# Single PSUM banks for the maxima of each FoX head, earlier loads of the FoX weights, and w_out's blocks subtracted on VectorE

## The chip, the cores and the metric

One core of one Trainium2 chip runs the whole program. The metric is the device time of one execution in microseconds (us); lower is better. The engines are named as in the profile: PE is TensorE's matmuls, PEld its weight loads, DVE is VectorE, ACT is ScalarE, POOL is GpSimd, SP is SyncE, whose queue issues every DMA of this kernel.

## The reference

One decoder layer over 2048 tokens of width 1024, with 16 learned meta tokens ahead of them. Three mixers (FoX attention, GLA, RG-LRU) read one input projection, and an output projection follows:

```python
hn = rms_norm(h, pre_g[l])
proj = hn @ w_in[l]
(fq, fk, fv, ff, fg, gq, gk, gv, ga, gg, lx, lg) = split_projection(proj)
...
# FoX: 8 heads of 64; c = cumsum(log_sigmoid(ff + b_f))
s = jnp.einsum('bhqd,bhkd->bhqk', qi, kf) * scale + cqi[..., None] - c[:, :, None, :]
mask = (kpos[None, :] <= qpos[:, None]) & valid[None, :]
p = jax.nn.softmax(jnp.where(mask, s, NEG), axis=-1)
y_fox = jnp.einsum('bhqk,bhkd->bhqd', p, vf) * jax.nn.silu(fg)
...
y = jnp.concatenate([y_fox, y_gla, y_lru], axis=-1) * vmask
h = h + rms_norm(y @ w_out[l], post_g[l])
```

## The kernel before, in words

The program is one long list of jobs in a fixed order: GLA (two pairs of heads, four chunks of 512 tokens each), RG-LRU (eight blocks of 128 channels), FoX (four pairs of heads, p = 0 to 3, four chunks of 512 queries each, c = 0 to 3), then the output projection. `merge` interleaves two generators: the mixing part of one job (for FoX `fox_attend`) and the preparing part of the next (`fox_prepare`). A scheduler then turns this list into one order for each engine by its own model of the time; each engine runs its order strictly in turn. Tiles come from rings of a fixed number of buffers; a new tile waits until the last reader of the tile whose place it takes is done.

The layout of FoX. The two heads of a pair lie on the upper and lower 64 partitions of the tiles KA (keys, high and low half), QA (queries) and KX. A product over one head's 64 channels therefore uses one half of the rows of PE's 128 x 128 array, and the products of the two heads use different halves.

`fox_prepare` projects keys (`fox_keys`), queries and values (`fox_values`, 24 matmuls of 128 x 128 for each block, line 503) and computes, for each block of 128 queries (i = 0 to 3) and each chunk pc of keys up to the diagonal, the largest score of each query: two products of the heads into the PSUM tile `mq` (line 1224), on the diagonal a mask added by a matmul (line 1228), and one reduction for each head on DVE (line 1232), which adds the decays CB and takes the maximum. `mq` is a tile of two banks, one bank for each head, and there is one such tile. The maxima of a chunk are transposed through the bank `fx` (line 1244), split on ACT and DVE and sent into QA by six small DMAs (line 1255).

`fox_attend` computes for each block j of 128 keys the scores of both heads (line 1284, six products with KA and two with KX; line 1290 the mask), the exponential on ACT into `pt` (line 1292), running sums `za` on DVE and POOL (lines 1296 to 1300), and the product with the values into the bank `fv` (line 1308; float32, the two heads in different halves of the columns of the array). At the end of a chunk the sums go through `fx` (line 1319) and through HBM to the normaliser `rz` (lines 512 to 521, 1326), POOL multiplies (lines 1315, 1327) and the result is stored to `yD` (line 1328).

Weights. Each group of 128 columns of w_in is loaded as a `raw` tile of 512 KB (line 418, ring of 4), squared and summed on ACT (line 465), and converted to two float16 halves on ACT and DVE (lines 436, 437) by `load_end`, which `post` calls at the start of the next job. For FoX the load of fk and fv of the next pair is in the list at chunk 0, its squares at chunk 1; fq and fg at chunks 2 and 3; each of these DMAs is queued behind `k.mark`, the last store to `yD` or the last of the six DMAs into QA, whichever the list had last.

Beside FoX runs `wout_ready`, in steps spread over the sixteen FoX jobs: it loads w_out in 32 blocks `wr` (256 KB) for their squares, loads them again, subtracts blocks from one another (`minus`, line 1381, 32 of 128 x 512), and converts them into the staging tile `ws` (lines 1447, 1448), which is stored to `wD` (line 1388). The output projection reads `wD`.

Of the kernel before, what the change touches and what calls it, by code (L numbers as in the profile page):

```python
# [9 lines left out]
F32 = mybir.dt.float32  # L10
# [6 lines left out]
ALU = mybir.AluOpType  # L17
# [70 lines left out]
class Ctx:  # L88
# [6 lines left out]


BUFS = {"A0": 3, "A2": 3, "KA": 6, "KB": 6, "QA": 2, "QB": 2, "B0": 2, "B1": 2, "B2": 2, "B3": 2, "V": 6, "G": 2, "R": 1,
        "T": 3, "ZZ": 8, "WR": 8, "WT": 2, "WS": 3, "TS": 12, "WC": 1, "OO": 3, "OX": 2, "LV": 5, "AT": 2, "AC": 2, "GV": 6, "GG": 6, "GS": 6, "M": 1, "MV": 1, "YG": 2, "RS": 2, "ZS": 1, "ZA": 2, "PT": 6, "ED": 2, "KT": 1, "Z": 1, "WH": 1, "WL": 1, "XC": 4, "X": 16, "L0": 4, "L1": 4, "L2": 2, "L3": 2, "L4": 6}


def unit(k, tag, shape, dt=F32, name=None):
# [8 lines left out]
    return ap  # L110


PBUFS = {"pj": 2, "mx": 2, "st": 2, "pv": 2, "fx": 1, "fv": 1}


def bank(k, tag="pj"):
# [292 lines left out]
def load_begin(k, nm):  # L409
    load_dma(k, nm)  # L410
    load_squares(k)


def load_dma(k, nm):
    cols, src = (48, k.ins["w_fa"]) if nm == "fa" else (P, k.ins["w_grp"][GROUPS[nm]])
    raw = k.wp.tile([P, KT, P], F32, name="raw", bufs=RAWB)[:, :, 0:cols]
    with k.tc.issue_after(k.mark) if nm[0] in ("fk", "fv", "fq", "fg") else nullcontext():
        k.nc.sync.dma_start(out=raw, in_=src)
    k.sent.append((nm, raw, cols))

# [20 lines left out]
def post(k, n=1):  # L441

    while k.begun:
        load_end(k)
    for _ in range(min(n, len(k.todo))):
        nm = k.todo.pop(0)
        if nm is None:
            load_squares(k)
        elif nm[0] == "load":
            load_dma(k, nm[1])  # L450
        else:
            load_begin(k, nm)


def fox_loads(p):

    return {0: [("load", ("fk", p)), ("load", ("fv", p))], 1: [None, None],
            2: [("load", ("fq", p)), ("load", ("fg", p))], 3: [None, None]}


def squares(k, tiles, scale=1.0):
# [647 lines left out]
def fox_begin(k, p):  # L1109

    nc = k.nc
    d = k.st["k", p] = Ctx()
    d.hi, d.lo, d.cb, d.V = [], [], [], []
    d.x = k.wk.tile([P, SEQ], BF16, name="KX", tag="KX", bufs=2)
    last = unit(k, "M", [P, 7 * NM], name="last")
    d.last = [last[:, NM // 2 * i:NM // 2 * (i + 1)].bitcast(F16) for i in range(2)]
    lx = last[:, NM:NM // 2 * 3].bitcast(BF16)
    lc = last[:, NM * 2:NM * 4].rearrange("p (h t) -> p h t", h=2)
    with k.tc.issue_after(k.pool):
        nc.gpsimd.memset(d.x, 1.0)  # L1120
# [12 lines left out]
    d.x = [d.x[:, CH * c:CH * c + CH] for c in range(NCH)] + [lx]
# [35 lines left out]
def fox_values(k, p, c):  # L1169
    nc = k.nc  # L1170
    wv = k.w["fv", p]
    m, nb = (P, 4) if c < NCH else (NM, 1)
    V = unit(k, "V" if c < NCH else "MV", [m, nb, P], name="fv")
    ps = blocks(bank(k))
    for i in range(nb):
        proj_tm(k, ps[0:m, i, :], wv, CH * c + P * i, m)
        yield
    nc.scalar.activation(V[0:m, :, :], ps[0:m, 0:nb, :], AF.Copy, scale=wv[2][0:m])
    k.st["k", p].V.append(V)
# [12 lines left out]
def fox_prepare(k, p, c):  # L1192
# [23 lines left out]
    for i in range(4):  # L1216
        for pc in range(c + 2 if i == 3 else c + 1):
            n = NM if pc > c else CH if pc < c else min(CH, NM + P * (i + 1))

            d0, d1, off = (P - NM, P, 0) if pc > c else (0, min(P, CH - NM - P * i), NM + P * i)  # L1220
            ps = pair(k, "mq")
            for h in range(2):
                hs = slice(64 * h, 64 * h + 64)
                nc.tensor.matmul(out=ps[:, h, 0:n], lhsT=qh[hs, P * i:P * i + P], rhs=d.hi[pc][hs, 0:n],  # L1224
                                 start=True, stop=pc < c)
            for h in range(2):
                if pc >= c:
                    nc.tensor.matmul(out=ps[:, h, off:off + d1 - d0], lhsT=k.identb, rhs=k.triq[:, d0:d1],
                                     start=False, stop=True)
            for h in range(2):  # L1230
                junk = k.wk.tile([P, 2, CH], BF16, name="mj", tag="MJ", bufs=1)
                nc.vector.tensor_tensor_reduce(out=junk[:, h, 0:n], in0=ps[:, h, 0:n], in1=d.cb[pc][:, h, 0:n],  # L1232
                                               scale=1.0, scalar=-3e38, op0=ALU.add, op1=ALU.max,
                                               accum_out=mp[:, 4 * h + i, pc:pc + 1])
            yield
            if next(rest, 0) is None:
                yield
    mm = small(k, "mm", [P, 8], bufs=2)
    nc.vector.tensor_reduce(mm, mp, axis=AX.X, op=ALU.max)
    for _ in range(1):  # L1240
        if next(rest, 0) is None:
            yield
    ps = bank(k, "fx")
    nc.tensor.transpose(out=ps[0:8, 0:P], in_=mm, identity=k.ident)

    mr = k.wk.tile([8, P], F32, name="mr", tag="MR", bufs=1)
# [16 lines left out]
def fox_attend(k, p, c):  # L1263
# [49 lines left out]
    o = unit(k, "R", [P, CH], name="fo")  # L1313
    nc.scalar.copy(out=o, in_=pv)
    nc.gpsimd.tensor_tensor(o, o, gate, op=ALU.mult)
    zp = bank(k, "fx")
    for h in range(2):
        hs = slice(64 * h, 64 * h + 64)
        nc.tensor.matmul(out=zp[hs, :], lhsT=k.ones[:, 0:64], rhs=za[h], start=True, stop=True)
# [18 lines left out]
def wout_ready(k):  # L1338
# [35 lines left out]
    for i, (q, j) in enumerate(groups):  # L1374
        (b11, b12, b22, b21), ahead = ahead, []
        if i + 1 < len(groups):
            ahead = [load(groups[i + 1][0], b, groups[i + 1][1]) for b in (0, 2, 3, 1)]

        def minus(x, y):
            t = k.wk.tile([P, KT // 2, P], F32, name="wt", tag="WT", bufs=BUFS["WT"])  # L1380
            nc.gpsimd.tensor_tensor(t, x, y, op=ALU.subtract)
            return t

        def put(nm, x):
            hl = stage()
# [261 lines left out]
```

## Time and profile before

| | |
|---|---|
| median of 3 runs | 2018.9 us (2014.85 to 2019.87) |
| the profiled execution, its own time | 2016.83 us |
| its span from the first to the last instruction | 2015.1 us |
| mean granted clock of TensorE | 0.976 of full speed |
| busy share of PE / DVE / ACT / POOL | 94% / 63% / 50% / 31% |
| from the first `mq` product to the first product of the output projection | 899.0 to 1702.2 us |

A share is busy time over the span. PE's busy time counts a matmul from its start to its modelled end. "Idle before" in a row is the time in which the engine had nothing to run before that instruction, with the instruction whose end let it go on.

### The profile page before, as it was taken

The page shows a single profiled execution, that of the slowest core. Times are in us where ns is not written, and L with a number is a line of the kernel's source. Part 1 is how long each engine was busy: PE and PEld are TensorE (multiplying, and loading weights), DVE is VectorE, ACT ScalarE, POOL GpSimd, SP SyncE. Part 2 cuts the span into 40 slices and gives each one's busy share as a digit, 9 for nine tenths or more (in the row PEclk, how much of TensorE's full clock was granted, in tenths as well). Part 3 has the DMA queues.
Part 4 walks back from the last instruction along what each step waited for, and adds up shares of the span by engine and source line. Part 5 has one row for each costly group of instructions (what it writes and reads, how often), then busy time and mean ns, then how long its engine had stood idle before and what let it go on. Part 6 is the DMA issues. An engine that isn't in the chain of part 4 may idle for free.

```text
span 2015.1 us, 39446 instructions
## 1 busy us (share of the span) xinstructions
PE 1893.3 (94%) x15988; PEld 985.4 (49%) x15988; DVE 1265.8 (63%) x2802; ACT 1011.9 (50%) x1561; POOL 630.7 (31%) x596
## 2 busy tenths in 40 slices
PE   6888999999999999989989998999899998999998
PEld 5456666665555555555434442344335432444443
DVE  7666363445788778673665367746874675567764
ACT  7655553344888887752345333433443335444441
POOL 3434232322433344330112113322332124343432
PEclk9889899999999999999999999999999998999999
DMA  7200120211211110101131104321232108733411
GB/s 226 70 7 29 41 86 28 74 44 34 74 43 45 44 41 22 63 20 64 38 116 48 54 12 135 95 77 64 90 116 70 43 23 303 218 116 115 136 43 63
DMA packets 116135, 152.70 MB, mean 76 GB/s; under 512 B 18792, under 2 KB 75816, under 8 KB 115952
## 3 DMA queue, kind: packets, MB, share of 16 engines
q1 hardware_dynamic: 115952, 150.18, 23.4%
q8 instruction: 125, 2.05, 0.4%
q14 instruction: 58, 0.48, 0.1%
HBM read 108.71 MB, written 41.33 MB: 74 GB/s over the span
## 4 chain that ended last, share of the span: by engine, by line
PE 66%; DVE 8%; DMA 5%; ACT 5%; issue 4%; POOL 4%; SPq 1%; POOLq 0%; ACTq 0%; DVEq 0%
PE pj L491 26%; PE pj L1576 14%; PE pj L503 5%; PE fv L1308 5%; PE sq L1284 4%; PE mq L1224 2%; DMA raw<-in_w_grp_dram 2%; PE st L596 1%; DMA rz<-rowD 1%; DVE mj L1232 1%; PE gs L1034 1%; DMA rowD<-consts 1%; PE pv L1068 1%; DVE xc L569 1%; POOL v L618 1%
## 5 line engine op out<-in xcount | busy, mean ns | idle before, releaser
L491 PE MATMUL pj<-xhl,whl 128*128 128x512 f16 (+3 forms) x3960 | 808.9, 355 | 10.0 <-ACT whl L436 7.7
L491 PEld LDWEIGHTS <-whl 128*128 128x128 f16 x3984 | 363.9, 98 | 393.9 <-issue 68.5
L1292 ACT ACTIVATE pt<-sq,consts 128x1024 f32<-128x1024 f32 (+4 forms) x176 | 163.4, 928 | 255.2 <-PE sq L1290 101.9
L1300 POOL TENSOR_TENSOR za<-za,pt 128x512 f32<-128x512 f32 (+1 forms) x80 | 99.4, 1243 | 503.3 <-ACT pt L1292 442.3
L1232 DVE CUSTOM_DVE_ANT_0 mj<-mq,CB 128x512 bf16<-128x512 f32 (+4 forms) x344 | 189.5, 579 | 57.0 <-PE mq L1224 28.5
L1576 PEld LDWEIGHTS <-whl 128*128 128x128 f16 x1344 | 130.7, 98 | 161.2 <-issue 4.9
L503 PEld LDWEIGHTS <-xhl 128*128 128x128 f16 (+1 forms) x3264 | 191.3, 99 | 32.5 <-issue 28.2
L503 PE MATMUL pj<-whl,xhl 128*128 128x128 f16 (+1 forms) x3024 | 196.1, 223 | 0.0
L1300 DVE TENSOR_TENSOR za<-za,pt 128x512 f32<-128x512 f32 (+3 forms) x208 | 135.6, 675 | 91.8 <-ACT pt L1292 84.6
L1308 PE MATMUL fv<-pt,fv 128*64 128x512 f32 (+4 forms) x704 | 174.7, 534 | 0.6 <-DVE QA L1106 0.6
L1576 PE MATMUL pj<-xhl,whl 128*128 128x512 f16 x768 | 169.1, 381 | 0.0
L1284 PE MATMUL sq<-QA,KA 64*128 64x512 f16 (+4 forms) x1032 | 128.4, 345 | 14.3 <-ACT pt L1292 11.8
L1576 PE MATMUL pj<-ts,whl 128*128 128x512 f16 x576 | 125.7, 379 | 0.0
L569 DVE SCALAR_TENSOR_TENSOR xc<-lx,consts,xc 128x448 f32<-128x448 f32 (+1 forms) x120 | 94.0, 783 | 3.5
L1560 POOL TENSOR_TENSOR o<-o,xt 128x512 f32<-128x512 f32 x31 | 51.6, 1683 | 120.3 <-issue 91.7
L1542 ACT ACTIVATE sqo<-o 128x512 bf16<-128x512 f32 x32 | 20.1, 630 | 129.5 <-DVE o L1536 129.5
L527 ACT ACTIVATE gate<-pj,consts 128x512 f32<-128x512 f32 (+2 forms) x72 | 46.1, 641 | 71.6 <-PE pj L491 62.5
L1284 PEld LDWEIGHTS <-KA 64*128 64x128 f16 (+1 forms) x1032 | 40.6, 94 | 84.0 <-issue 62.0
L1224 PE MATMUL mq<-KA,QA 64*128 64x512 f16 (+4 forms) x344 | 61.4, 346 | 21.3 <-DVE consts L1232 19.1
L604 POOL TENSOR_TENSOR v<-a 128x448 f32<-128x448 f32 (+1 forms) x40 | 39.0, 976 | 134.1 <-ACT a L602 134.1
L1582 DVE SCALAR_TENSOR_TENSOR o<-pj,consts,o 128x512 f32<-128x512 f32 x56 | 41.0, 744 | 60.0 <-PE pj L1576 55.8
L1284 PE MATMUL sq<-QA,KX 64*128 64x512 bf16 (+4 forms) x344 | 66.6, 342 | 4.1 <-DMA QA<-dr 4.1
(253 smaller groups left out, 2810.8 us busy)
## 6 DMA issues: line engine op xcount, KB each, us to landing
raw<-in_w_grp_dram SPq DMA_DIRECT2D x44, 512.0 KB
wr<-in_w_out_dram SPq DMA_DIRECT2D x64, 256.0 KB
y<-yD SPq DMA_DIRECT2D x32, 512.0 KB
wD<-ws SPq DMA_DIRECT2D x56, 256.0 KB
CB<-c32D SPq DMA_DIRECT2D x32, 256.0 KB
xhl<-wD SPq DMA_DIRECT2D x16, 512.0 KB
xt<-in_x_dram SPq DMA_DIRECT2D x16, 512.0 KB
out_dram<-o SPq DMA_DIRECT2D x32, 256.0 KB
```

Of the source, the lines that this page charges most:

```text
L491: nc.tensor.matmul(out=ps, lhsT=a[:, kt, 0:m], rhs=b[:, kt, u0:u0 + n], start=i == 0, stop=i == 23)
L503: nc.tensor.matmul(out=ps, lhsT=a[:, kt, u0:u0 + m], rhs=b[:, kt, :], start=i == 0, stop=i == 23)
L527: k.act = nc.scalar.activation(out, ps, AF.Tanh, scale=hinv).ins
L569: nc.vector.scalar_tensor_tensor(out=xc, in0=lx[:, j:j + n], scalar=cw(j), in1=xc, op0=ALU.mult, op1=ALU.add)
L1224: nc.tensor.matmul(out=ps[:, h, 0:n], lhsT=qh[hs, P * i:P * i + P], rhs=d.hi[pc][hs, 0:n], start=True, stop=pc < c)
L1232: nc.vector.tensor_tensor_reduce(out=junk[:, h, 0:n], in0=ps[:, h, 0:n], in1=d.cb[pc][:, h, 0:n], scale=1.0, scalar=-3e38, op0=ALU.add, op ...
L1284: nc.tensor.matmul(out=sp[0:m, h, off:], lhsT=a[j // 4][hs, kk], rhs=b[hs, off:], start=i == 0, stop=i == 3 and d < 0)
L1292: k.exp = nc.scalar.activation(pt[0:m, :, off:], sp[0:m, :, off:], AF.Exp, scale=K.esc[0:m]).ins
L1300: eng.tensor_tensor(out=za[h][0:m, off:], in0=za[h][0:m, off:], in1=pt[0:m, h, off:], op=ALU.add)
L1308: nc.tensor.matmul(out=pv[hs, off1:], lhsT=V1[0:m1, j1 % 4, hs], rhs=pt1[0:m1, h, off1:], start=j1 == 0, stop=j1 == nj - 1)
L1560: eng.tensor_tensor(out=o, in0=o, in1=xt[:, h, :], op=ALU.add)
L1576: nc.tensor.matmul(out=ps, lhsT=a[:, kt, :], rhs=w[b + kt // 4][:, :, kt % 4, :], start=kt + j == 0, stop=(kt, j) == (KT - 1, 2))
```

## The change

`minus` runs on DVE in place of POOL. The rings of `wr` and `ws` shrink from 8 to 6 and from 3 to 2. FoX's weights get a ring of their own, `rawf`, of three tiles; load, squares and conversion of a group are asked for together (fk and fv at chunk 1, fq and fg at chunk 3), and only those of the first pair are queued behind `k.mark`. In `fox_prepare` each head takes a single bank of a ring of three named `mq`, from which the transposes of the maxima and the sums of `za` take their bank too; the two-bank tile and `fx` go. The values of the last 16 tokens move into the tile `last`.

```diff
-        "T": 3, "ZZ": 8, "WR": 8, "WT": 2, "WS": 3, ...
+        "T": 3, "ZZ": 8, "WR": 6, "WT": 2, "WS": 2, ...
...
-PBUFS = {"pj": 2, "mx": 2, "st": 2, "pv": 2, "fx": 1, "fv": 1}
+PBUFS = {"pj": 2, "mx": 2, "st": 2, "pv": 2, "mq": 3, "fv": 1}
...
-    raw = k.wp.tile([P, KT, P], F32, name="raw", bufs=RAWB)[:, :, 0:cols]
-    with k.tc.issue_after(k.mark) if nm[0] in ("fk", "fv", "fq", "fg") else nullcontext():
+    fox = nm[0] in ("fk", "fv", "fq", "fg")
+    raw = k.wp.tile([P, KT, P], F32, name="rawf" if fox else "raw", bufs=3 if fox else RAWB)[:, :, 0:cols]
+    with k.tc.issue_after(k.mark) if fox and nm[1] == 0 else nullcontext():
...
-    return {0: [("load", ("fk", p)), ("load", ("fv", p))], 1: [None, None],
-            2: [("load", ("fq", p)), ("load", ("fg", p))], 3: [None, None]}
+    return {1: [("fk", p), ("fv", p)], 3: [("fq", p), ("fg", p)]}
...
-            ps = pair(k, "mq")
+            ps = [bank(k, "mq") for _ in range(2)]
             for h in range(2):
                 hs = slice(64 * h, 64 * h + 64)
-                nc.tensor.matmul(out=ps[:, h, 0:n], lhsT=qh[hs, P * i:P * i + P], rhs=d.hi[pc][hs, 0:n],
+                nc.tensor.matmul(out=ps[h][:, 0:n], lhsT=qh[hs, P * i:P * i + P], rhs=d.hi[pc][hs, 0:n],
                                  start=True, stop=pc < c)
...
-    ps = bank(k, "fx")
+    ps = bank(k, "mq")
     nc.tensor.transpose(out=ps[0:8, 0:P], in_=mm, identity=k.ident)
...
-    zp = bank(k, "fx")
+    zp = bank(k, "mq")
...
-            nc.gpsimd.tensor_tensor(t, x, y, op=ALU.subtract)
+            nc.vector.tensor_tensor(t, x, y, op=ALU.subtract)
```

PE's order is the same up to the first chunk of FoX and through the output projection, and differs in between; the changed program's line numbers are 5 or 6 lower (line 418 alone is now 419). PE, the second step of the first chunk (272 keys), before: both heads, then both masks.

```order
L503 MATMUL pj<-whl,xhl 128x128
L1224 LDWEIGHTS QA
L1224 MATMUL mq<-KA,QA 128x272
L1224 LDWEIGHTS QA
L1224 MATMUL mq<-KA,QA 128x272
L1228 LDWEIGHTS consts
L1228 MATMUL mq<-consts 128x128
L1228 LDWEIGHTS consts
L1228 MATMUL mq<-consts 128x128
L503 LDWEIGHTS xhl
```

The same place now; the rows left out are 18 products of the values (`pj`, line 497).

```order
L1219 LDWEIGHTS QA
L1219 MATMUL mq<-KA,QA 128x272
L1223 LDWEIGHTS consts
L1223 MATMUL mq<-consts 128x128
L497 LDWEIGHTS xhl
L497 MATMUL pj<-whl,xhl 128x128
...
L1219 LDWEIGHTS QA
L1219 MATMUL mq<-KA,QA 128x272
L1223 LDWEIGHTS consts
L1223 MATMUL mq<-consts 128x128
```

The second head's product and mask have moved 18 products of the values behind the first head's. PE again, in the second chunk of the first pair, where `fox_attend` multiplies with the values, before: one row holds both heads (x2).

```order
L1290 LDWEIGHTS consts
L1290 MATMUL sq<-consts 128x128
L1308 MATMUL fv<-pt,fv 64x400 x2
L491 LDWEIGHTS whl
L491 MATMUL pj<-xhl,whl 128x512
```

The same place now.

```order
L1285 LDWEIGHTS consts
L1285 MATMUL sq<-consts 128x128
L1303 MATMUL fv<-pt,fv 64x400
L1219 LDWEIGHTS QA
L1219 MATMUL mq<-KA,QA 128x400
L1223 LDWEIGHTS consts
L1223 MATMUL mq<-consts 128x128
L1303 MATMUL fv<-pt,fv 64x400
L485 LDWEIGHTS whl
```

One head's maximum product and its mask now stand between the two heads' products with the values. Over the whole of FoX the program before has 176 pairs of heads at line 1224, of which one is not back to back, and 171 at line 1308, of which 24 are not; now 95 and 48 are not. The order of PE changes its kind of instruction (128 rows, 64 rows, 64 columns, float32 or not) 882 times before and 964 times now.

SP, where the loads of fk and fv of a later pair stand, before: behind the store of a chunk (line 1328).

```order
L521 DMA rowD<-consts 128x8
L1326 DMA rz<-rowD 64x512 x2
L1328 DMA yD<-fo 128x512
L418 DMA raw<-in_w_grp_dram 128x1024 x2
L1346 DMA wr<-in_w_out_dram 128x512 x6
```

Now one such pair of loads stands ahead of the normaliser's round trip.

```order
L1250 DMA QA<-dr 1x4x128 x6
L508 DMA rowD<-zs 1x512 x2
L419 DMA rawf<-in_w_grp_dram 128x1024 x2
L510 DMA consts<-rowD 128x8
L515 DMA rowD<-consts 128x8
```

No load of these now follows a store of line 1323 directly, and seven of the sixteen stand ahead of the first of the six DMAs into QA, where four did.

## Rows read from the trace of the kernel before

**Rows 1.** The page, busy time of each engine, share of the span, count.

```profile
span 2015.1 us, 39446 instructions
PE 1893.3 (94%) x15988; PEld 985.4 (49%) x15988; DVE 1265.8 (63%) x2802; ACT 1011.9 (50%) x1561; POOL 630.7 (31%) x596
```

**Rows 2.** Windows: length, busy us (count) by engine, clock, DMA share, GB/s.

```profile
899.00:1702.00 803.00, 754.39 (x5605) 321.78 (x5603) 488.25 (x1339) 310.99 (x455) 195.79 (x153) 0.98 0.25 80
```

**Rows 3.** Waits of PE in 899:1702: total us, times, longest.

```profile
PE mq L1224 <- DVE consts L1232: 19.1, 20, 3.4
PE sq L1284 <- ACT pt L1292: 11.8, 13, 3.6
PE sq L1284 <- DMA QA<-dr: 4.1, 3, 2.4
...
PE pj L491 <- DVE whl L437: 0.2, 1, 0.2
```

**Rows 4.** Timeline of PE at 935.0 and 1475.2: start, us, shape.

```profile
935.04 0.39 PE L1224 MATMUL mq<-KA,QA 64*128 64x512 f16 x2
935.36 0.62 PE L503 MATMUL pj<-whl,xhl 128*128 128x128 f16 x8
...
1475.20 0.89 PE L503 MATMUL pj<-whl,xhl 128*128 128x128 f16 x13
1476.02 0.39 PE L1284 MATMUL sq<-QA,KX 64*128 64x512 bf16 x1
1476.34 0.82 PE L491 MATMUL pj<-xhl,whl 128*128 128x512 f16 x3
```

**Rows 5.** Timeline of PE at 1501.2 and 1510.3 (line 1308: two records a product).

```profile
1501.28 0.82 PE L1284 MATMUL sq<-QA,KA 64*128 64x512 f16 x6
1501.94 0.38 PE L1284 MATMUL sq<-QA,KX 64*128 64x512 bf16 x2
1502.25 1.08 PE L1308 MATMUL fv<-pt,fv 128*64 128x512 f32 x4
1503.26 0.34 PE L503 MATMUL pj<-whl,xhl 128*128 128x128 f16 x3
...
1510.79 1.07 PE L1308 MATMUL fv<-pt,fv 128*64 128x512 f32 x2
1511.79 0.61 PE L1284 MATMUL sq<-QA,KA 64*128 64x512 f16 x4
```

**Rows 6.** The chain that ended last, 1425:1450: start, us, what.

```profile
1433.96 0.33 SPq L1328
...
1434.39 4.37 DMA raw<-in_w_grp_dram
...
1440.00 1.01 ACT pt L1292
...
1441.05 1.04 PE sq L1284 x8
```

**Rows 7.** Timeline of PE, the instructions after five waits [idle before].

```profile
1024.68 0.61 PE L1284 MATMUL sq<-QA,KA 64*128 64x512 f16 x4 [3.03 <-ACT pt L1292]
1139.89 0.29 PE L1224 MATMUL mq<-KA,QA 64*128 64x272 f16 x2 [1.34 <-DVE consts L1232]
1232.26 0.41 PE L1224 MATMUL mq<-KA,QA 64*128 64x272 f16 x2 [3.37 <-DVE consts L1232]
1348.26 0.29 PE L1224 MATMUL mq<-KA,QA 64*128 64x272 f16 x2 [2.42 <-DVE consts L1232]
1441.05 0.39 PE L1284 MATMUL sq<-QA,KA 64*128 64x512 f16 x2 [3.63 <-ACT pt L1292]
```

**Rows 8.** Groups by form in 899:1702: busy us, mean ns, idle before.

```profile
L1300 DVE TENSOR_TENSOR za<-za,pt 128x512 f32<-128x512 f32 x120 | 99.2, 850 | 52.2 <-ACT pt L1292 45.4 <-POOL za L1300 6.2
...
L1381 POOL TENSOR_TENSOR wt<-wr 128x512 f32<-128x512 f32 x16 | 24.1, 1508 | 4.4 <-DMA wr<-in_w_out_dram 4.4
L1381 POOL TENSOR_TENSOR wt<-wr,wt 128x512 f32<-128x512 f32 x16 | 23.5, 1467 | 0.3
...
L1297 DVE TENSOR_TENSOR za<-pt 128x512 f32<-128x512 f32 x24 | 15.5, 687 | 21.3 <-ACT pt L1292 21.3
...
L512 ACT COPY zs<-fx 128x512 f32<-128x512 f32 x15 | 8.8, 586 | 20.7 <-PE fx L1319 20.7
```

More of the change, by code (lines that the diff above doesn't have):

```diff
@@ L97 @@
 BUFS = {"A0": 3, "A2": 3, "KA": 6, "KB": 6, "QA": 2, "QB": 2, "B0": 2, "B1": 2, "B2": 2, "B3": 2, "V": 6, "G": 2, "R": 1,
-        "T": 3, "ZZ": 8, "WR": 8, "WT": 2, "WS": 3, "TS": 12, "WC": 1, "OO": 3, "OX": 2, "LV": 5, "AT": 2, "AC": 2, "GV": 6, "GG": 6, "GS": 6, "M": 1, "MV": 1, "YG": 2, "RS": 2, "ZS": 1, "ZA": 2, "PT": 6, "ED": 2, "KT": 1, "Z": 1, "WH": 1, "WL": 1, "XC": 4, "X": 16, "L0": 4, "L1": 4, "L2": 2, "L3": 2, "L4": 6}
+        "T": 3, "ZZ": 8, "WR": 6, "WT": 2, "WS": 2, "TS": 12, "WC": 1, "OO": 3, "OX": 2, "LV": 5, "AT": 2, "AC": 2, "GV": 6, "GG": 6, "GS": 6, "M": 1, "MV": 1, "YG": 2, "RS": 2, "ZS": 1, "ZA": 2, "PT": 6, "ED": 2, "KT": 1, "Z": 1, "WH": 1, "WL": 1, "XC": 4, "X": 16, "L0": 4, "L1": 4, "L2": 2, "L3": 2, "L4": 6}
 def unit(k, tag, shape, dt=F32, name=None):
@@ L445, in post @@
     for _ in range(min(n, len(k.todo))):
[L446 to L452, printed above, removed]
+        load_begin(k, k.todo.pop(0))
 def fox_loads(p):
-    return {0: [("load", ("fk", p)), ("load", ("fv", p))], 1: [None, None],
-            2: [("load", ("fq", p)), ("load", ("fg", p))], 3: [None, None]}
+    return {1: [("fk", p), ("fv", p)], 3: [("fq", p), ("fg", p)]}
 def squares(k, tiles, scale=1.0):
@@ L1114, in fox_begin @@
     d.x = k.wk.tile([P, SEQ], BF16, name="KX", tag="KX", bufs=2)
-    last = unit(k, "M", [P, 7 * NM], name="last")
+    last = unit(k, "M", [P, 7 * NM + P], name="last")
+    d.lastV = last[:, 7 * NM:].rearrange("p (b v) -> p b v", b=1)
     d.last = [last[:, NM // 2 * i:NM // 2 * (i + 1)].bitcast(F16) for i in range(2)]
@@ L1172, in fox_values @@
     m, nb = (P, 4) if c < NCH else (NM, 1)
-    V = unit(k, "V" if c < NCH else "MV", [m, nb, P], name="fv")
+    V = unit(k, "V", [m, nb, P], name="fv") if c < NCH else k.st["k", p].lastV
     ps = blocks(bank(k))
@@ L1227, in fox_prepare @@
                 if pc >= c:
-                    nc.tensor.matmul(out=ps[:, h, off:off + d1 - d0], lhsT=k.identb, rhs=k.triq[:, d0:d1],
+                    nc.tensor.matmul(out=ps[h][:, off:off + d1 - d0], lhsT=k.identb, rhs=k.triq[:, d0:d1],
                                      start=False, stop=True)
@@ L1231, in fox_prepare @@
                 junk = k.wk.tile([P, 2, CH], BF16, name="mj", tag="MJ", bufs=1)
-                nc.vector.tensor_tensor_reduce(out=junk[:, h, 0:n], in0=ps[:, h, 0:n], in1=d.cb[pc][:, h, 0:n],
+                nc.vector.tensor_tensor_reduce(out=junk[:, h, 0:n], in0=ps[h][:, 0:n], in1=d.cb[pc][:, h, 0:n],
                                                scale=1.0, scalar=-3e38, op0=ALU.add, op1=ALU.max,
```

## Prediction

> **What bounds the kernel now.** I read the page first: PE is busy for 94% of the span, DVE for 63%, ACT for 50%, POOL for 31% [rows 1]. Then the window of the stage that the change touches, from the first `mq` product to the first product of the output projection: 803.0 us, of which PE is busy 754.4 [rows 2]. So PE sets the time here too, and 48.6 us is all that any removed wait can give back in this stage. The list of PE's waits in the same window says what that idle time is: eleven kinds, 47.6 us together, the largest the `mq` products that wait for a reduction on DVE (19.1 us in 20 waits) and the score products that wait for the exponential on ACT (11.8 us in 13) [rows 3]. The reader should keep both numbers apart: what the change does to PE's 754 us of work, and what it does to the 48 us of waits.
>
> **What PE's work costs, and what the new order does to it.** The timeline shows that the two heads of a pair run at the same time. A pair of 512-column products at line 1224 starts at 935.04 and the next product starts at 935.36: 0.32 us for two heads. One head alone, at 1476.02, is followed at 1476.34: 0.32 us as well [rows 4]. Half of PE's rows then do nothing. Three pairs in a row take 0.66 us, from 1501.28 to 1501.94, or 0.22 a pair [rows 5]; so 0.10 of the 0.32 is the change to the next kind of product. The entry costs as much: 13 products of the values take 0.89 us and 8 take 0.62, 0.054 for each more, so the last of the 13 starts at about 1475.85, and the lone product at 1476.02, 0.12 later than the next value product would [rows 4]. The Trainium skill, "TensorE: Matmul & The Clock Gate", section "Why this matters for your kernels", says that a small-K product alone takes the time of a full one and that the gain is only in running several at once; this trace agrees (0.32 against 0.32 us). By that rule alone the split `mq` pairs would cost about 14 us; the rows add the price of changing kinds.
>
> At line 1308 (float32, the heads in two halves of the columns) both heads take 1.01 us, from 1502.25 to 1503.26, and one head alone 1.00 us, from 1510.79 to 1511.79 [rows 5]. A split pair costs a full second pass.
>
> Now the counts, from the two orders. A head's bank is free for the first head while the second still waits for its own, so the scheduler sends the first head ahead and puts other work between. At line 1224, 95 pairs are no longer back to back (one before); the lone heads hold 65,088 columns against 1,024. At line 1308, 48 pairs are split (24 before), with 38,176 lone columns against 19,616. PE's order changes kind 82 times more.
> - `mq`: half of the 64,064 added columns is time that used to overlap, 32,032 / 512 x 0.22 = 13.8 us. Lower bound 0, if the lone heads all stood in a wait of PE; no upper doubt, the count is fixed.
> - `fv`: 9,280 / 512 x 1.00 = 18.1 us.
> - changes of kind: 82 x 0.10 = 8.2 at most, 0 if they fall in waits; I take 6, since most follow work that keeps PE full.
>
> Together 38 us of added work for an engine that is 94% busy in this stage.
>
> **What the waits give back.** *The loads.* The chain that ended last shows a load of FoX weights with all that follows: the store of line 1328 issues at 1433.96, the load behind it in SP's queue takes 4.37 us, ACT squares it, the exponential comes after that on ACT, and the score products start at 1441.05 [rows 6], after 3.63 us in which PE had nothing to run [rows 7]. Such a load, queued behind a chunk's store, occurs five times, and after each of them PE stands: 3.03, 1.34, 3.37, 2.42 and 3.63 us, 13.8 together [rows 7]. Three of the five are counted as waits for DVE, because DVE in its turn waits for the sum of squares. In the changed order every load of the later pairs is issued about a chunk or more before its squares, so these stalls should go: 13 us; bounds 0 (a load that waits for one of the three tiles holds SP's queue and all the small DMAs behind it) and 13.8.
>
> *The three banks.* Of the 19.1 us of `mq` waits, 7.1 belong to the loads; 12.0 are left for the banks. I take half, 6: a third bank lets one product go ahead, but DVE still takes one maximum after the other. Bounds 0 and 12.
>
> *The subtractions.* 32 on POOL at 1,508 and 1,467 ns are 47.6 us off POOL. On DVE the nearest row is the first addition of a chunk, the same size and type, 687 ns [rows 8]: 22 us onto DVE, which is idle for 315 of the 803 us [rows 2]. Against that, DVE's other additions of this size take 850 ns on average [rows 8], 163 more than that row; POOL works on the same sums meanwhile. 120 of them are 20 us of stretch, and the subtractions are 47.6 of POOL's 195.8 us [rows 2], so some 5 us come back. DVE ends up with 17 us more, under its idle time. If the cover were gone, those 17 us would stand before `mq` maxima; if DVE is relieved more, up to 5 us of waits go. I take 0, bounds -5 and +8.
>
> *Smaller rings, the shared ring.* A third staged block within the time that a store of `ws` takes would now hold ACT; two fewer `wr` tiles load later. The trace of before has neither wait; the nearest row is the 4.4 us for which POOL waited once for `wr` [rows 8]. Bounds 0 and 6, I take 0: the scheduler has put the blocks as far apart as before on ACT. The sums of `za` take a bank of the `mq` ring until ACT has copied it, 0.59 us and sixteen times [rows 8]: at most 16 x 0.59 = 9 us, 0 if other work fills it; 0, because projections follow each time.
>
> **Sum.** 13.8 + 18.1 + 6 - 13 - 6 = +18.9 us on the profiled execution's 2016.83 (span 2015.1 and 1.7 around it): 2035.7, that is 2036. The profiled execution lies 2.1 us below the median of 2018.9, which I leave in the range.
>
> **The rivals.**
> - *No change.* All of the loads' and the banks' waits go (13.8 + 12.0), the exponential's remaining 5.1 us too, and the changes of kind fall in waits (0 for 8): 31.9 - 30.9 = +1, so 2018. For it: the waits sit where the split heads now sit. Against it: DVE's speed has not changed, and it ends 12 us of these waits.
> - *Faster.* The lone heads fall into the time in which PE used to wait for both maxima, so the 13.8 us at line 1224 cost nothing; `fv` alone costs, 18.1, and 26 to 31 us of waits go: -8 to -13, so 2004 to 2009. It decides from the point where PE's idle time in the stage falls below some 10 us of the 48 and the `mq` products are still no longer in sum. The trace speaks against it: the waits are 20 in number, three of them from the loads, while 94 more pairs are split. The Trainium skill, "SBUF — State Buffer", section "SBUF: two separate sides", says that DVE with two SBUF inputs and POOL lock each other out for whole instructions; the 850 ns against 687 agree with that. By that rule moving the subtractions could free DVE of more than my 5 us, which would help this rival by at most the 12 us that DVE ends.
> - *Slower still.* The shared ring and the smaller rings make new waits: `za`'s 9 us and the staging's 6, with a third of the loads' gain lost to loads that wait for a tile: 2036 + 9 + 6 + 4 = 2055. It decides when the transposes and the sums wait for a maximum's bank in most chunks.
> - *The loads do not come earlier*, because SP runs its queue in turn and a stalled store stands ahead of them: 13 us less given back, 2049.
>
> **Chances.** Forecast 0.52 (its own range 2028 to 2046), the two slower cases together 0.21, no change 0.15, faster 0.12. A difference of 0.3%, 6 us, is about what a measurement of this kernel can tell from none. The forecast's low end of 2028 is slower than 2018.9 by more than that, so slower has 0.52 + 0.21 = 0.73, same 0.15, faster 0.12. The range leaves out 1 in 10 at each end: 2012 (inside the faster case) to 2053 (inside the slower ones).
>
> **What would show each step.** In the profile of the changed kernel: PE's busy time in the stage up by some 30 us and the stage longer than 803; products of one head at line 1219 with shapes x1 in the timeline, 0.32 us to the next; the records at line 1303 with longer total time; no waits of ACT for `rawf` and no gap of PE of 2 to 4 us after a load; `mq` waits of about 6 us; DVE some 15 to 20 us busier and POOL some 48 less. The prediction is wrong if PE's busy time hardly rises (then a lone head is cheaper than rows 4 and 5 say), or if the waits of the stage fall to less than 10 us, or if new waits for a bank, a `ws` tile or a `rawf` tile appear.

## The result, and the profile after

The changed kernel takes 2037.3 us (median of 4 runs, 2034.52 to 2037.73) against 2017.5 for the kernel before on the same chip (4 runs, 2014.85 to 2019.87): a ratio of 1.0097, 95% interval 1.0085 to 1.011. It is slower by about 1%, as forecast (2036, range 2012 to 2053).

The page of the changed kernel, the two lines that answer to [rows 1]: span, then busy time of each engine, share and count.

```profile
span 2036.0 us, 39502 instructions
PE 1926.5 (95%) x15988; PEld 995.9 (49%) x15988; DVE 1268.1 (62%) x2834; ACT 1009.9 (50%) x1561; POOL 578.5 (28%) x564
```

The span grew by 20.9 us, PE's busy time by 33.2 with the same 15,988 matmuls. The window of the FoX stage, from the first `mq` product to the first product of the output projection, answers to [rows 2]: length, busy us (count) of PE, PEld, DVE, ACT and POOL, granted clock, DMA share, GB/s.

```profile
899.00:1724.00 825.00, 787.21 (x5605) 331.36 (x5606) 491.68 (x1368) 306.41 (x450) 146.32 (x120) 0.99 0.25 77
```

The stage holds all of the loss: 825.0 us against 803.0. The same 5,605 matmuls keep PE busy for 32.8 us more, and PE's idle time falls from 48.6 to 37.8, by 10.8. 32.8 - 10.8 = 22.0. POOL is 49.5 us less busy and DVE only 3.4 more, although it has taken over the subtractions.

The list of PE's waits in the same window answers to [rows 3]: total us, times, longest.

```profile
PE mq L1219 <- DVE consts L1227: 11.9, 16, 2.3
PE sq L1279 <- ACT pt L1287: 11.9, 17, 2.3
...
PE sq L1279 <- DMA QA<-dr: 0.7, 1, 0.7
...
PE pj L485 <- ACT whl L437: 0.2, 1, 0.2
```

The waits of the `mq` products fell by 7.2 us, those for the DMAs into QA by 3.4; the waits for the exponential are as long as before (11.9 against 11.8).

The timeline of PE shows the split heads: start, us, shape. The first three rows answer to [rows 4], the last four to [rows 5].

```profile
944.81 0.39 PE L1219 MATMUL mq<-KA,QA 64*128 64x512 f16 x1
945.13 0.60 PE L485 MATMUL pj<-xhl,whl 128*128 128x512 f16 x2
945.67 0.39 PE L1219 MATMUL mq<-KA,QA 64*128 64x512 f16 x1
...
1462.50 1.07 PE L1303 MATMUL fv<-pt,fv 128*64 128x512 f32 x2
1463.50 0.39 PE L1219 MATMUL mq<-KA,QA 64*128 64x512 f16 x1
1463.82 1.07 PE L1303 MATMUL fv<-pt,fv 128*64 128x512 f32 x2
1464.82 0.39 PE L1219 MATMUL mq<-KA,QA 64*128 64x512 f16 x2
```

A lone `mq` head holds PE from 944.81 to 945.13, 0.32 us, and its partner comes 0.86 later. At 1462.50 one head's product with the values takes 1.00 us, then comes an `mq` product of 0.32, and then a single head's product with the values again takes 1.00: 2.00 for two heads, where a pair takes 1.01 [rows 5]. (Line 1308 has 704 records, two a product, so the pairs there are 176 and not 171; 24 of them before and 48 now are not back to back.)

### The profile page after: what moved, and what is told of

The parts are those of the page before. It is cut to its first block, busy times and chain, and to the rows that moved or that the text cites. A ratio compares the mean times of both kernels' runs of the same rounds, so it can differ in the third digit from the quotient of the medians.

```text
span 2036.0 us, 39502 instructions
## 1 busy us (share of the span) xinstructions
PE 1926.5 (95%) x15988; PEld 995.9 (49%) x15988; DVE 1268.1 (62%) x2834; ACT 1009.9 (50%) x1561; POOL 578.5 (28%) x564
## 5 line engine op out<-in xcount | busy, mean ns | idle before, releaser
L1227 DVE CUSTOM_DVE_ANT_0 mj<-mq,CB 128x512 bf16<-128x512 f32 (+4 forms) x344 | 190.4, 578 | 34.6 <-PE mq L1223 20.8
L497 PEld LDWEIGHTS <-xhl 128*128 128x128 f16 (+1 forms) x3264 | 192.0, 100 | 33.2 <-issue 29.6
L1303 PE MATMUL fv<-pt,fv 128*64 128x512 f32 (+4 forms) x688 | 194.1, 540 | 2.5 <-DVE QA L1100 1.8
L1295 DVE TENSOR_TENSOR za<-za,pt 128x512 f32<-128x512 f32 (+3 forms) x208 | 125.6, 624 | 99.0 <-ACT pt L1287 96.5
L1279 PE MATMUL sq<-QA,KA 64*128 64x512 f16 (+4 forms) x1032 | 128.8, 339 | 12.1 <-ACT pt L1287 11.9
L1219 PE MATMUL mq<-KA,QA 64*128 64x512 f16 (+4 forms) x344 | 85.4, 343 | 13.8 <-DVE consts L1227 11.9
L1537 ACT ACTIVATE sqo<-o 128x512 bf16<-128x512 f32 x32 | 20.2, 630 | 134.0 <-DVE o L1531 132.0
L522 DVE SCALAR_TENSOR_TENSOR gate<-gate,pj 128x512 f32<-128x512 f32 (+2 forms) x72 | 45.2, 627 | 51.9 <-ACT gate L521 51.8
L598 POOL TENSOR_TENSOR v<-a 128x448 f32<-128x448 f32 (+1 forms) x40 | 38.8, 969 | 127.7 <-ACT a L596 127.6
L1219 PEld LDWEIGHTS <-QA 64*128 64x128 f16 x352 | 24.0, 93 | 103.9 <-issue 90.4
```

Of the source, the lines that this page charges most:

```text
L497: nc.tensor.matmul(out=ps, lhsT=a[:, kt, u0:u0 + m], rhs=b[:, kt, :], start=i == 0, stop=i == 23)
L522: nc.vector.scalar_tensor_tensor(out=out, in0=out, scalar=1.0, in1=ps, op0=ALU.add, op1=ALU.mult)
L1219: nc.tensor.matmul(out=ps[h][:, 0:n], lhsT=qh[hs, P * i:P * i + P], rhs=d.hi[pc][hs, 0:n], start=True, stop=pc < c)
L1227: nc.vector.tensor_tensor_reduce(out=junk[:, h, 0:n], in0=ps[h][:, 0:n], in1=d.cb[pc][:, h, 0:n], scale=1.0, scalar=-3e38, op0=ALU.add, op ...
L1279: nc.tensor.matmul(out=sp[0:m, h, off:], lhsT=a[j // 4][hs, kk], rhs=b[hs, off:], start=i == 0, stop=i == 3 and d < 0)
L1295: eng.tensor_tensor(out=za[h][0:m, off:], in0=za[h][0:m, off:], in1=pt[0:m, h, off:], op=ALU.add)
```

## The experiments

In all runs the kernel before ran on the same chip: medians 2019.2 (17 runs) for the first four, 2020.0 (20 runs) for the next four, 2019.9 (7 runs) for the last two. Its single runs spread from 2012 to 2027, so ratios are what to compare. The table takes PE's busy and idle time from the window of the FoX stage in each profile (idle is length less busy), us; each row is one profiled execution. "Lower clock" is the time of that window in which TensorE's granted clock was 0.50, the lower of its two levels (1.2 GHz); in the rest it was 1.00 (2.4 GHz).

| kernel | stage | PE busy | PE idle | lower clock | median | ratio (95%) |
|---|---|---|---|---|---|---|
| before | 803.0 | 754.4 | 48.6 | 27.3 | 2017.5 | 1 |
| subtractions (e8) | 795.5 | 756.0 | 39.5 | 20.4 | 2014.7 | 0.9969 (0.9954 to 0.9985) |
| loads, rings (e3) | 793.9 | 751.9 | 42.0 | 20.5 | 2010.3 | 0.9957 (0.9941 to 0.9973) |
| loads, rings, subtractions (e1) | 799.6 | 755.6 | 44.0 | 27.3 | 2011.1 | 0.9954 (0.9936 to 0.9972) |
| loads, subtractions (e7) | 792.7 | 749.5 | 43.2 | 13.7 | 2008.4 | 0.9943 (0.9924 to 0.9963) |
| banks (e2) | 823.4 | 787.6 | 35.8 | 13.7 | 2040.4 | 1.0106 (1.0086 to 1.0126) |
| banks, subtractions (e9) | 818.3 | 783.7 | 34.6 | 10.2 | 2035.0 | 1.0079 (1.0056 to 1.0102) |
| banks, loads, rings (e10) | 824.3 | 791.2 | 33.1 | 13.7 | 2039.0 | 1.0102 (1.007 to 1.0133) |
| the whole change | 825.0 | 787.2 | 37.8 | 10.2 | 2037.3 | 1.0097 (1.0085 to 1.011) |
| e1 with masks between heads (e4) | 819.4 | 776.3 | 43.1 | 20.5 | 2033.3 | 1.0066 (1.0043 to 1.0088) |
| e1 with values head by head (e5) | 812.9 | 769.6 | 43.3 | 27.3 | 2023.4 | 1.002 (1.0008 to 1.0033) |
| two single banks and fx (e6) | 831.2 | 801.2 | 30.0 | 10.2 | 2047.5 | 1.0137 (1.0113 to 1.0161) |

The profiled execution of e1 took 2020.56 us, 9 above its median, so its row shows some us more than an execution at the median would. The mean granted clock in these windows was 0.98 (before, e1, e5) or 0.99 (all others); a hundredth of 780 us is 8 us, so a few us of busy time between two rows should be read beside the column of the lower clock. The kernels with the banks lost time although they have a higher clock than the one before: 10.2 or 13.7 us at the lower level against 27.3.

### e1: the changed program without the banks

```diff
-PBUFS = {"pj": 2, "mx": 2, "st": 2, "pv": 2, "mq": 3, "fv": 1}
+PBUFS = {"pj": 2, "mx": 2, "st": 2, "pv": 2, "fx": 1, "fv": 1}
...
-            ps = [bank(k, "mq") for _ in range(2)]
+            ps = pair(k, "mq")
...
-    ps = bank(k, "mq")
+    ps = bank(k, "fx")
...
-    zp = bank(k, "mq")
+    zp = bank(k, "fx")
```

> The change with its banks undone: the two-bank tile and the bank fx are back, the earlier loads, the smaller rings and the subtractions on DVE stay. Theory (the split heads cost some 33 us of PE's work, the rest gives back some 11 us of waits or a little more): PE's order has no split mq pair and 23 split fv pairs, so PE's busy time in the FoX stage falls back to about 755 us and the run takes 2003 to 2010 us, 0.4 to 0.7% faster than before. Rival (the loss comes from the loads, the rings or the subtractions, and the banks are harmless): 2030 to 2040 us, as the whole change.

Measured 2011.1 us. PE's order has no split pair of the maxima any more, and 23 of the values. The rival is out; the theory's upper end was missed by 1 us. All of the loss is the banks'; what is left of the change is a gain of some 9 us.

### e2: the banks alone

The lines of e1's diff the other way round, in the kernel before.

> The kernel before with the three single banks alone. Theory: 89 split mq pairs (34,384 columns of first heads), 50 split fv pairs (22,272 columns, 11,344 before), 97 more changes of kind, so 14.6 + 21.3 + up to 10 us of added work on PE, less some 5 us of mq waits: 2045 to 2058 us, slower than the whole change, whose loads give some 11 us back. Rival (the banks pay for themselves): 2012 to 2020 us.

Measured 2040.4. The rival is out, but the theory was 5 us too high at its lower end. The window of the stage says why.

```profile
902.00:1725.40 823.40, 787.62 (x5604) 330.18 (x5603) 476.94 (x1339) 309.74 (x455) 191.34 (x153) 0.99 0.25 78
```

PE is busy for as long as in the whole change, and idle for 35.8 us only, although the loads still come behind the stores. The last of the five stalls [rows 6, 7] shows how. ACT's timeline at this load, with the idle time before it in brackets:

```profile
1447.49 1.06 ACT L465 ACTIVATE whl<-raw 128x1024 bf16<-128x1024 f32 x1 [6.20 <-DMA raw<-in_w_grp_dram]
1448.45 0.19 ACT L465 ACTIVATION_READ_ACCUMULATOR whl<-raw 128x1 f32 x1
1448.54 1.09 ACT L1292 ACTIVATE pt<-sq,consts 128x1024 f32<-128x1024 f32 x1
```

PE's timeline over the same time:

```profile
1443.81 0.37 PE L1224 MATMUL mq<-KA,QA 64*128 64x512 f16 x1 [2.34 <-DVE consts L1232]
...
1444.74 1.14 PE L1284 MATMUL sq<-QA,KA 64*128 64x512 f16 x5
1445.67 0.32 PE L1224 MATMUL mq<-KA,QA 64*128 64x144 f16 x1
...
1446.68 1.97 PE L1308 MATMUL fv<-pt,fv 128*64 128x512 f32 x4
...
1449.69 0.82 PE L1284 MATMUL sq<-QA,KA 64*128 64x512 f16 x6 [0.22 <-ACT pt L1292]
```

ACT stands for 6.20 us for the load, longer than before, and then does the exponential late. PE has a list of other products meanwhile, and waits 0.22 us for that exponential in place of 3.63. The 2.34 us in front of the first row are another wait, for a reduction on DVE, which ends before the load has landed, so not all of the 3.63 us is gained. Over the stage ACT waits 21.1 us for loads here and 21.9 before; the first wait of PE behind the five loads is 1.52, none, 1.74, 1.30 and 0.22 us, 4.8 in place of 13.8 [rows 7]. The pair of products with the values at 1446.68 lies in a stretch of granted clock 0.50 (1445.1 to 1448.5) and takes 1.97 us, where one at the upper level takes 1.08 [rows 5].

### e3: the loads and the rings alone

The whole change without the banks (e1's diff) and with this:

```diff
-            nc.vector.tensor_tensor(t, x, y, op=ALU.subtract)
+            nc.gpsimd.tensor_tensor(t, x, y, op=ALU.subtract)
```

> The earlier loads with the ring rawf and the smaller rings wr and ws, but banks and subtractions as before. Theory (each of the five loads behind a store stalls PE, 13.8 us together): no gap of PE of 2 to 4 us after a load, ACT waits for no weights, 2002 to 2008 us. Rival (PE only waits elsewhere, or the smaller rings take it back): 2014 to 2022 us.

Measured 2010.3: a gain, but of some 9 us, less than the theory's 11 to 17. PE's idle time fell by 6.6. Its busy time is 2.5 lower, about what the 6.8 us less at the lower clock account for. The rival is out, but one half of it shows at the third of the five loads. There ACT squares the weights at 1202.85 and 1209.05 without waiting for them, and PE waits at the same two products as before all the same: first ACT, then PE.

```profile
1222.24 0.72 ACT L1442 ACTIVATE ws<-wr,consts 128x512 f16<-128x512 f32 x1 [2.72 <-DMA wr<-in_w_out_dram]
```

```profile
1224.41 0.39 PE L1219 MATMUL mq<-KA,QA 64*128 64x512 f16 x2 [2.32 <-DVE consts L1227]
...
1231.41 0.29 PE L1219 MATMUL mq<-KA,QA 64*128 64x272 f16 x2 [2.34 <-DVE consts L1227]
```

In the kernel before these two waits were 2.17 us (at 1224.72) and 3.37 us [rows 7]; in e1 one of 4.10 us is left, in e7 they are 4.19 and 1.20. In e3 it is a block of w_out that ACT waits for there, and not a weight of FoX. At the other four places the products of [rows 7] wait for nothing, 10.4 us less, and other waits for DVE grew: 1.23 us near the first place and 1.80 near the last.

### e4: the order broken without any change of banks

The change without the banks, with each head's mask asked for behind its product, so that 80 pairs at the diagonal have a mask between them.

```diff
             for h in range(2):
                 hs = slice(64 * h, 64 * h + 64)
                 nc.tensor.matmul(out=ps[:, h, 0:n], lhsT=qh[hs, P * i:P * i + P], rhs=d.hi[pc][hs, 0:n],
                                  start=True, stop=pc < c)
-            for h in range(2):
                 if pc >= c:
```

> As e1_pairs_back, but on the diagonal each head's product is followed by its own mask, so that the 80 pairs with masks are no longer back to back, with the two-bank tile and thus every wait for DVE unchanged. This prices a lone head alone. Theory: 21,504 columns at 0.22 us for 512 are 9.2 us, 156 more changes of kind at 0.10 us are 15.6 us, so 20 to 26 us above e1_pairs_back. Rival (a lone head costs nothing, what counts is the waits): within 4 us of e1_pairs_back.

Measured 2033.3, 22.2 above e1. PE's timeline, four rows at the first chunk of the stage:

```profile
899.63 0.34 PE L1219 MATMUL mq<-KA,QA 64*128 64x400 f16 x1
899.90 0.23 PE L1222 MATMUL mq<-consts 128*128 128x128 bf16 x1
900.06 0.34 PE L1219 MATMUL mq<-KA,QA 64*128 64x400 f16 x1
900.33 0.23 PE L1222 MATMUL mq<-consts 128*128 128x128 bf16 x1
```

Each head takes its 0.27 us alone, and every mask pays its own entry (0.16 us from 899.90 to 900.06, where one more product of 128 columns in a row of its kind costs 0.054). The stage is 19.8 us longer than e1's, PE is busy for 20.7 more and idle for 0.9 less, with 6.8 us less at the lower clock. So the order by itself costs what was said, with the same bytes, banks and waits; and it takes next to nothing from the waits.

### e5: the products with the values split

The change without the banks, and the products that end a chunk asked for head by head.

```diff
-            for j1, m1, off1, pt1, V1 in todo[:1] if j < nj - 1 else todo:
-                for h in range(2):
+            for h in range(2):
+                for j1, m1, off1, pt1, V1 in todo[:1] if j < nj - 1 else todo:
```

> The changed program with pairs of banks again (2011.1 us when it ran), in which the products with the values that end a chunk are asked for head by head in place of block by block: 129 pairs of heads stand back to back instead of 159, and 11,712 more columns run alone. Theory (a lone head at the float32 product takes the time of both): 5,856 / 512 x 1.00 = 11.4 us more, and up to 2.8 for 28 changes of kind: 2021 to 2026. Rival (the end of a chunk is where PE waits for the exponential anyway, so lone heads are hidden there): 2010 to 2015.

Measured 2023.4, 12.3 above e1's median (13.3 by the two ratios); PE is busy for 14.0 us more, idle for 0.7 less. The theory holds and the rival is out: the second pass is not hidden at the end of a chunk.

### e6: two single banks in place of three

```diff
-PBUFS = {"pj": 2, "mx": 2, "st": 2, "pv": 2, "mq": 3, "fv": 1}
+PBUFS = {"pj": 2, "mx": 2, "st": 2, "pv": 2, "mq": 2, "fx": 1, "fv": 1}
...
-    ps = bank(k, "mq")
+    ps = bank(k, "fx")
...
-    zp = bank(k, "mq")
+    zp = bank(k, "fx")
```

> The changed program with two single banks for the maxima in place of three, and the bank fx back for the transposes and the sums. Theory (the order is broken by each head having a tile of its own; the third bank only takes waits away): 112 pairs of the maxima and 57 of the values are not back to back, against 95 and 48, and the kind changes 72 times more, so some 3 + 8 + 7 us above the changed program's 2037: 2048 to 2060. Rival (the third bank is what lets the first head run ahead, or the shared ring is what costs): 2012 to 2037.

Measured 2047.5, half a us below the theory's range and far outside the rival's. The window of the stage:

```profile
897.20:1728.40 831.20, 801.23 (x5604) 332.82 (x5605) 493.29 (x1368) 305.72 (x448) 147.05 (x120) 0.99 0.24 76
```

A bank for each head breaks the pairs, with two banks more than with three (14.0 us more of PE's time). But one half of the theory finds no support, that the third bank takes waits away: with two PE is idle for 30.0 us, with three for 37.8, and the `mq` waits are 6.2 us against 11.9. This run doesn't isolate the third bank, because PE's order changed too (more split pairs leave PE more to do) and the transposes and sums have `fx` to themselves.

### e7: the rings as before

```diff
-"WR": 6, "WT": 2, "WS": 2,
+"WR": 8, "WT": 2, "WS": 3,
```

in e1's program.

> The changed program with pairs of banks again, and the rings of wr and ws at 8 and 3 as before. PE's order has the same count of pairs and changes as with 6 and 2. Theory (the smaller rings cost nothing): 2008 to 2014, as with the smaller rings (2011.1). Rival (two fewer wr and one fewer ws make ACT and DVE wait): up to 6 us less, 2004 to 2007.

Measured 2008.4 against e1's 2011.1; the intervals of the two ratios overlap, so the smaller rings' cost lies between nothing and a few us. This is the lowest median of all kernels here, ahead of the one before (0.9943) and the changed one; its interval overlaps those of e1 and e3.

### e8: the subtractions alone

e3's line the other way round, in the kernel before.

> The kernel before with the subtractions on DVE and nothing else. Theory (they lie under DVE's idle time, and part of the time comes back because POOL no longer works beside DVE's additions): within 4 us of the kernel before; in the stage DVE 10 to 17 us busier, POOL 46 to 48 less. Rivals: the maxima come later behind them, 5 to 10 us more; or DVE is relieved by as much as it takes on and the waits fall, 4 to 8 us less.

Measured 2014.7, 5.4 us less: the theory missed by 1.4, and the second rival holds. The window of the stage:

```profile
904.80:1700.30 795.50, 755.97 (x5606) 321.09 (x5605) 492.22 (x1371) 311.23 (x455) 150.16 (x121) 0.99 0.25 80
```

And the groups by form that answer to [rows 8]: busy us, mean ns, idle before.

```profile
L1300 DVE TENSOR_TENSOR za<-za,pt 128x512 f32<-128x512 f32 x120 | 92.7, 796 | 48.9 <-ACT pt L1292 43.7 <-POOL za L1300 4.8
...
L1381 DVE TENSOR_TENSOR wt<-wr,wt 128x512 f32<-128x512 f32 x16 | 11.9, 744 | 0.0
...
L1381 DVE TENSOR_TENSOR wt<-wr 128x512 f32<-128x512 f32 x16 | 11.6, 727 | 0.5 <-DMA wr<-in_w_out_dram 0.5
```

DVE takes on 11.9 + 11.6 = 23.5 us and is 4.0 us busier than before, not 10 to 17: 19.5 came back. The additions are 54 ns shorter each (6.5 us), and the conversions into the staging tile, which also read two tiles of 128 x 512, 109 and 131 ns:

```profile
L1448 DVE SCALAR_TENSOR_TENSOR ws<-wt,consts,ws 128x512 f16<-128x512 f32 x32 | 28.5, 892 | 6.8 <-ACT ws L1447 6.7
L1448 DVE SCALAR_TENSOR_TENSOR ws<-wr,consts,ws 128x512 f16<-128x512 f32 x24 | 20.3, 847 | 2.0 <-ACT ws L1447 1.7
```

In the kernel before these two groups had 1,001 and 978 ns:

```profile
L1448 DVE SCALAR_TENSOR_TENSOR ws<-wt,consts,ws 128x512 f16<-128x512 f32 x32 | 32.0, 1001 | 6.6 <-ACT ws L1447 6.6
L1448 DVE SCALAR_TENSOR_TENSOR ws<-wr,consts,ws 128x512 f16<-128x512 f32 x24 | 23.5, 978 | 3.4 <-ACT ws L1447 3.1
```

Additions and conversions make some 13 of the 19.5 us; the rest is spread over smaller groups and was not followed. The reductions at line 1232, which read one of their two tiles from PSUM, took 685 ns in both. PE's idle time falls from 48.6 to 39.5. The five waits of [rows 7] are 2.78, 1.32, 1.31, 1.06 and 2.61 us in this run, 9.1 in place of 13.8: half of what the subtractions take from PE's idle time (4.7 of 9.1 us) comes out of the waits that the loads take too.

### e9 and e10: the banks with one other part each

e9 is e2 with the subtractions on DVE, e10 is the whole change with them on POOL (e3's line, in either direction).

> The kernel before with the three single banks and the subtractions on DVE; loads and rings as before. 94 pairs of the maxima and 44 of the values are not back to back and the kind changes 960 times, so PE's work in the stage should be 3 to 4 us less than with the banks alone (787.6). Theory (each edit takes from the same waits of PE, and with the banks alone these are already down to 35.8 us): idle time of PE in the stage 34 to 38 us, whole time 2033 to 2038. Rival (the edits take different waits; the subtractions alone took 9.1 us): idle 25 to 29, whole time 2024 to 2030.

> The changed program with the subtractions on POOL: the three banks, the loads and the rings. 90 pairs of the maxima and 56 of the values are not back to back and the kind changes 988 times, so PE's work in the stage should be some 9 us above the changed program's 787. Theory (each edit takes from the same waits of PE): idle time of PE in the stage 34 to 38 us, whole time 2044 to 2049. Rival (the edits take different waits; the loads alone took 6.6 us from PE's idle time): idle 27 to 31, whole time 2036 to 2041.

The windows of the stage, e9 first:

```profile
903.40:1721.70 818.30, 783.67 (x5604) 329.89 (x5603) 494.18 (x1370) 309.58 (x454) 148.30 (x120) 0.99 0.25 79
```

and e10:

```profile
899.00:1723.30 824.30, 791.23 (x5603) 331.12 (x5604) 478.98 (x1336) 305.46 (x448) 193.63 (x152) 0.99 0.24 76
```

e9 fits the theory in idle time (34.6) and in time (2035.0), and its rival is out. e10 decides less: its idle time of 33.1 lies between the two ranges, nearer to the theory's, and its 2039.0 is in the rival's, since PE's added work came to 4 us and not to the 9 that I had counted. Taken together: alone the subtractions, the loads and the banks take 9.1, 6.6 and 12.8 us from PE's idle time, 28.5 if they added up. All three take 10.8. Each of these figures is one profiled execution's, and PE's order differs from one program to the next, so they show that the savings don't add and not which edit lost how much.

## Why the prediction was right, step by step

**The added work of PE, +38 by the sum.** Measured 32.8 in the stage. The mechanism is shown, not only argued: broken pairs without new banks cost 20.7 us of PE's time in e4 and 14.0 in e5, where the same prices gave 20 to 26 and 11 to 14. The sum looks 5 us high, but it had no term for TensorE's clock, which is higher in the changed kernel: over a whole execution the mean was 0.980 to 0.982 in its four, and 0.970 to 0.980 in the 44 of the kernel before that ran beside the experiments. The stretches of the stage in which the granted clock was 0.50, before (length, busy us of PE, PEld, DVE, ACT and POOL, clock, DMA share, GB/s, each cut by 0.1 us at both ends):

```profile
1026.20:1029.40 3.20, 3.20 (x14) 0.76 (x12) 1.78 (x7) 1.72 (x3) 1.52 (x1) 0.50 0.04 15
1231.00:1237.60 6.60, 5.34 (x22) 1.36 (x23) 5.24 (x12) 1.11 (x1) 1.64 (x1) 0.50 0.31 108
1442.60:1445.80 3.20, 3.20 (x15) 0.78 (x13) 2.79 (x8) 1.66 (x3) 1.77 (x1) 0.50 0.26 87
1661.10:1671.10 10.00, 6.29 (x24) 1.49 (x22) 1.55 (x3) 2.81 (x3) 0.00 (x0) 0.50 0.58 152
1698.60:1701.80 3.20, 3.20 (x14) 0.73 (x10) 3.20 (x5) 2.85 (x4) 0.00 (x0) 0.50 1.02 408
```

and in the changed kernel:

```profile
1237.70:1240.90 3.20, 3.20 (x7) 0.66 (x7) 3.20 (x7) 1.72 (x2) 1.44 (x1) 0.50 0.46 160
1708.70:1712.00 3.30, 3.30 (x12) 0.64 (x8) 1.00 (x2) 1.72 (x2) 1.54 (x1) 0.50 0.94 339
1719.00:1722.20 3.20, 3.20 (x14) 0.74 (x11) 2.99 (x8) 2.19 (x2) 0.00 (x0) 0.50 1.03 411
```

Each of the eight begins during or right behind a wait of PE of 1.59 to 3.63 us; the first three before belong to the waits of 3.03, 3.37 and 3.63 us [rows 7]. Not every such wait has one: none follows the 2.42 us at 1348.26. An estimate from these rows: if a product takes twice its time at the lower level (1.97 against 1.08 us in e2), half of PE's busy time there is the clock's, 11.1 us of 22.2 before and 5.1 of 10.2 now. PE's work at the upper level is then 743.3 us before and 782.1 now: +38.8, as the sum had it, with 6.0 us given back by the clock. The same estimate gives 24.5 us for e4 and 13.7 for e5. The first two terms and the changes of kind were not measured apart in the whole change, since their records overlap.

**The waits, -19 by the sum.** Measured 10.8. This is the step that was mis-sized, by 8 us. The 6 us of the clock, which the prediction put at nothing by having no term for it, made up for most of this: 38.8 - 10.8 - 6.0 = 22.0 us in the stage. That the whole time came out within 1 us of the forecast (+18.9 forecast, +19.8 by the medians) is in this part luck. The step failed in how it was built, as a sum of parts that each had their own waits:
- *The loads, -13.* Alone they gave PE's idle time 6.6 us (e3). The wait of 3.37 us was counted as the load's, and most of it stays when the load is early (2.34 us in e3). On top of the banks little is left for the loads: 2.7 us of idle time (e10 against e2) and nothing clear in the time (1.0102 against 1.0106), because the banks' order already had other products for PE while ACT waited for a load (e2). The prediction said that every later load would be issued about a chunk or more ahead of its squares, and that ACT would no longer wait for `rawf`. Neither came true for most of them. A load's DMA waits in SP's queue for a free tile of the ring of three, until the conversion at line 438 has read the old one:

```profile
SPq L419 <- DVE whl L438: 20.2, 4, 10.9
```

Four pairs of loads are issued 3.3 to 4.4 us ahead of their first square; one load comes 123 us ahead. ACT waits for `rawf` 11.1 us in 4 waits of the stage, against 21.9 in 8 before, of which 4.2 are the first pair's, now ahead of the window. PE mostly works through it: behind the first of the four waits, at 1010.54, it stands 1.13 us for an exponential, behind the others at most 0.32. The last one, as issued by SP, on ACT and on PE:

```profile
1294.51 1.59 SPq L419 DMA_DIRECT2D rawf<-in_w_grp_dram  x2
```

```profile
1298.26 1.06 ACT L459 ACTIVATE whl<-rawf 128x1024 bf16<-128x1024 f32 x1 [5.28 <-DMA rawf<-in_w_grp_dram]
```

```profile
1294.54 4.92 PE L485 MATMUL pj<-xhl,whl 128*128 128x512 f16 x22 [1.94 <-DVE consts L436]
1299.40 0.82 PE L1279 MATMUL sq<-QA,KA 64*128 64x512 f16 x6
```

The 1.94 us in front of the first row end with DVE's conversion of weights that had landed before.

- *The banks, -6.* Alone they took 12.8 us off PE's idle time, with the five waits of [rows 7] 9.0 us shorter (e2). The reason given, a third bank that lets one product go ahead, is not borne out: with two banks and `fx` PE is idle for less (e6). That a bank for each head gives PE something to do while a reduction is out fits e2 and e6, but no run shows it apart from the new order; the third bank keeps more pairs whole (95 split against 112). Which of the two heads' banks is free first at each place was not followed.
- *The subtractions, 0, bounds -5 and +8.* Alone -5.4 (e8), just beyond the bound that stood for a relieved DVE. The stretch that comes back was sized at 5 us, from the additions; it was 19.5. On top of the banks (e9 against e2) and of the loads (e1 against e3) the intervals of the ratios overlap, so what they are worth there is not settled. The Trainium skill, "SBUF — State Buffer", section "SBUF: two separate sides", has DVE with two SBUF inputs and POOL lock each other out; e8 agrees, with additions 54 and conversions 109 and 131 ns shorter and the reductions from PSUM unchanged. The prediction took from this rule that more than 5 us could come back, and more did.
- *Rings and shared ring, 0.* The rings cost at most a few us (e7). In the whole list of PE's waits in the changed stage there is none at the transposes (line 1239) or at the sums (line 1314), the two that now take a bank of the shared ring.

**The rivals.** *No change* and *faster* needed 26 to 31 us of waits to go; 10.8 went. *Faster* also had the lone heads fall into waits: e4 and e5 show that they don't. *Slower still* needed waits for the shared ring, which are not there on PE; its third part, loads that wait for a tile, is there. *Loads not earlier* came true in part, through the ring and not through a stalled store, and cost PE little.

**What would show each step.** PE up by some 30: 32.8. `mq` waits of about 6: 11.9. DVE 15 to 20 busier: 3.4. POOL 48 less: 49.5. Two of its signs went against it, in its own words: ACT waits for `rawf` (11.1 us), and new waits for a `rawf` tile appear (20.2 us of SP's queue). So the part on the loads was wrong although the time was right; PE's added work, which decides the time, was as said.

## What to carry to other kernels

A PSUM tile that both heads share is also what keeps their two products back to back; give each head a tile of its own and a scheduler can put other work between them, here at 95 of 176 pairs, and on a half-used array each head then cost a full pass (0.32 us alone, 0.32 as a pair). Before adding up what several edits take from waits, ask whether they take it from the same waits: here three edits worth 28.5 us of idle time one by one were worth 10.8 together, while the added work of the engine that bounds the stage counted in full, by the estimate above, once the clock is set apart. A removed wait can take a stretch at the lower clock with it, and that belongs in the sum: here 27.3 us at the lower level became 10.2. Edits of one change are best timed apart: this one held a gain of some 8 to 12 us inside a loss of 20.

## What the runs showed of the hardware

An elementwise operation moved from POOL to DVE cost DVE a sixth of its own time: 23.5 us of subtractions made DVE 4.0 us busier, because the additions (850 to 796 ns) and the conversions (1,001 and 978 to 892 and 847 ns) that ran beside it became shorter (e8); reductions that read one tile from PSUM stayed at 685 ns. The nearest row for such a move is therefore not the operation's duration alone but also the mean of the same engine's operations against that of its fastest group, 687 ns here [rows 8].
